# Seven of 22 gated pairs by a seven-product scheme

## The chip, the cores and the metric

One Trainium2 chip, one of its cores. The time is device microseconds of one launch: 893.27 us as the median of three runs (892.84 to 893.52). PE is TensorE, which does the matmuls; DVE is VectorE, ACT ScalarE, POOL GpSimd, SP the engine whose queue issues most transfers. Each engine takes its instructions in a written order and waits on semaphores for the others.

## What is computed

A decoder block over 16 meta tokens and 512 tokens of 1024 channels: a norm, one input projection, two mixers (a gated linear recurrence and a state-space mixer), one output projection, then the gated part that the change touches, and a last norm.

```python
def conv_glu_ffn(h, w_up, conv_w, conv_b, w_down):
    u = causal_dwconv(h @ w_up, conv_w, conv_b)      # 3 taps over tokens, per channel
    gate, val = jnp.split(u, 2, axis=-1)             # 2 x 2816 channels
    return (jax.nn.silu(gate) * val) @ w_down
...
h = h + conv_glu_ffn(rmsnorm(h, norm2_w[l]), ffn_w_up[l], ffn_conv_w[l],
                     ffn_conv_b[l], ffn_w_down[l])
y = rmsnorm(h, final_norm_w)
return y[:, N_META:, :]
```

All data are float32.

## The kernel before

Channels lie on the 128 partitions, tokens along the free axis. Every product is taken in three matmuls: weights and tokens are each split into a rounded high half (`hi`, float32r, written by ACT) and the rest (`lo`, written by DVE), and wh x xh + wh x xl + wl x xh is summed in PSUM (`product`, line 181).

The up-projection has 44 output tiles of 128 channels: tile j is a gate, tile 22 + j its value, a pair. For each tile, 8 blocks of 128 input channels, 3 matmuls each, in two halves of the tokens (258 and 256 of 514: two meta tokens are kept for the taps). `conv3` (line 790) multiplies the product by the tokens' norm factor `rstd2` (`fr`, DVE), and does the three taps: one on ACT with the bias, two on DVE (`fc`). The loop at line 806 adds `silu` on ACT, the gate's product on DVE, and at once the split of the result (`ac_hi` on ACT, `ac_lo` on DVE), from which the down-projection (`down`, line 818) reads: 8 output tiles, 22 blocks, 3 matmuls of 512 tokens each, the last tile in two halves.

Weights come in 512 KB pieces through SP's queue into three buffers (`raw`), are split into three buffers each of `whi` and `wlo`, and `weights` (line 176) keeps this two pieces ahead. A buffer is taken again when its last reader is through. PSUM has two pairs of banks (`pj`) for products of 514 tokens, and four single banks (`px`).

What sets the order: the program is written once, and a scheduler with priorities lays out a fixed order for each engine. Weight preparation runs under `first()`; `evac()` ranks above it; `tc.issue_after` puts an instruction behind another on its engine.

Of the kernel before, what the change touches and what calls it, by code (L numbers as in the profile page):

```python
# [54 lines left out]
def tile_block(ctx: ExitStack, tc: tile.TileContext, xT, w_in, w_dt, w_out, w_up, w_down,  # L55
               par, consts, consti, out, dbg=None):
    nc = tc.nc
    V, A, G, PE = nc.vector, nc.scalar, nc.gpsimd, nc.tensor
# [93 lines left out]

    def raw_tiles(key):
        name = "_".join(map(str, key))
        return (wp.tile([P, KD * P], F32, tag="raw", name=f"raw_{name}", bufs=3),
                wp.tile([P, KD * P], F32R, tag="whi", name=f"whi_{name}"),
                wp.tile([P, KD * P], F32R, tag="wlo", name=f"wlo_{name}"))
# [780 lines left out]
```

## Time and profile before

| | |
|---|---|
| median of three runs | 893.27 us (892.84 to 893.52) |
| the profiled execution | 892.85 us, span 890.7 us |
| PE, DVE, ACT busy | 98%, 62%, 47% of the span |
| mean granted TensorE clock | 0.997 |
| up-projection: first matmul, last product read out from | 505.4 us, 757.4 us |

Busy time of PE is no measure of its speed, since matmuls overlap: what counts is the distance between starts. The column "idle before" of a group is the engine's idle time before those instructions, with what ended it.

### The profile page before, as it was taken

The numbers are of one execution on the slowest core, as the hardware profiler recorded it, in microseconds if no ns is written. First come the engines' busy times: TensorE is split into PE (matmuls) and PEld (weight loads), VectorE is DVE, ScalarE is ACT, GpSimd is POOL, SyncE is SP. The second block draws the span as 40 slices with busy tenths as digits, with TensorE's granted clock in tenths as the row PEclk, the third lists the DMA queues.
The fourth block names the chain that finished last, engine by engine and source line by source line (L and its number), as shares of the span: only waits on it lengthen the run. The fifth ranks groups of instructions, "written<-read, shape, count | busy, mean of one in ns | idle before, by whom it ended". The sixth has DMA issues, their size and how long they took to land.

```text
span 890.7 us, 16334 instructions
## 1 busy us (share of the span) xinstructions
PE 871.0 (98%) x6936; PEld 831.4 (93%) x6936; DVE 553.9 (62%) x869; ACT 414.6 (47%) x625; POOL 23.8 (3%) x46
## 2 busy tenths in 40 slices
PE   7999999999999999999999999999999999999995
PEld 6998899999999999999999999999999999888885
DVE  6985968698776767454333367766666777433233
ACT  8629855866445444353222264444444444323221
POOL 1000000010000000000000000000000000000001
PEclk9999999999999999999999999999999999999998
DMA  7324332212211222244233333222232333233312
GB/s 245 91 96 163 125 97 71 72 48 70 71 58 67 95 72 72 84 153 145 95 96 95 95 93 96 84 88 93 95 96 95 96 95 90 83 88 107 89 43 94
DMA packets 29081, 84.65 MB, mean 95 GB/s; under 512 B 3128, under 2 KB 6712, under 8 KB 29008
## 3 DMA queue, kind: packets, MB, share of 16 engines
q1 hardware_dynamic: 26480, 80.02, 28.8%
q10 hardware_dynamic: 2528, 3.60, 1.3%
q8 instruction: 54, 0.88, 0.4%
q14 instruction: 19, 0.16, 0.1%
HBM read 81.45 MB, written 2.15 MB: 94 GB/s over the span
## 4 chain that ended last, share of the span: by engine, by line
PE 84%; ACT 4%; DVE 3%; DMA 1%; issue 1%; SPq 0%; DVEq 0%; ACTq 0%
PE pup L190 28%; PE pj L190 24%; PE pout L190 10%; PE pdn L823 5%; PE pdn L825 5%; PE pdn L824 5%; ACT L L467 1%; PE psu L441 1%; PE po L704 1%; PE po L703 1%; PE pa L686 1%; PE pS L674 1%; DMA ab<-acum_d 1%; DMA rs_d<-rh 1%; PE psx L429 1%
## 5 line engine op out<-in xcount | busy, mean ns | idle before, releaser
L190 PE MATMUL pj<-u_hi,whi_in 128*128 128x272 f32 (+1 forms) x752 | 156.1, 287 | 2.1 <-ACT z L512 1.4
L190 PE MATMUL pj<-u_hi,wlo_in 128*128 128x272 f32 (+1 forms) x752 | 156.6, 287 | 0.0
L190 PE MATMUL pj<-u_lo,whi_in 128*128 128x272 f32 (+1 forms) x752 | 155.9, 286 | 0.0
L190 PE MATMUL pup<-u2h,wlo_up 128*128 128x258 f32 x704 | 141.6, 282 | 0.0
L190 PE MATMUL pup<-u2h,whi_up 128*128 128x258 f32 x704 | 140.7, 282 | 0.0
L190 PE MATMUL pup<-u2l,whi_up 128*128 128x258 f32 x704 | 140.6, 281 | 0.0
L190 PEld LDWEIGHTS pj<-u_hi,whi_in 128*128 128x128 f32 x752 | 115.7, 188 | 5.2 <-issue 2.5
L190 PEld LDWEIGHTS pj<-u_lo,whi_in 128*128 128x128 f32 x752 | 116.0, 188 | 2.0 <-issue 1.5
L190 PEld LDWEIGHTS pj<-u_hi,wlo_in 128*128 128x128 f32 x752 | 116.5, 189 | 1.3 <-issue 1.2
L190 PEld LDWEIGHTS pup<-u2h,wlo_up 128*128 128x128 f32 x704 | 108.0, 188 | 0.1
L190 PEld LDWEIGHTS pup<-u2l,whi_up 128*128 128x128 f32 x704 | 108.0, 189 | 0.0
L190 PEld LDWEIGHTS pup<-u2h,whi_up 128*128 128x128 f32 x704 | 107.6, 188 | 0.0
L161 DVE TENSOR_TENSOR wlo_in<-raw_in,whi_in 128x1024 fp32r<-128x1024 f32 (+1 forms) x58 | 64.3, 1109 | 54.3 <-ACT whi_in L160 53.8
L160 ACT ACTIVATE whi_in<-raw_in 128x1024 fp32r<-128x1024 f32 (+1 forms) x58 | 56.0, 965 | 54.4 <-PE pj L190 41.0
L823 PE MATMUL pdn<-ac_hi,whi_dn 128*128 128x512 f32 (+1 forms) x198 | 73.1, 369 | 0.0
L824 PE MATMUL pdn<-ac_lo,whi_dn 128*128 128x512 f32 (+1 forms) x198 | 73.0, 368 | 0.0
L825 PE MATMUL pdn<-ac_hi,wlo_dn 128*128 128x512 f32 (+1 forms) x198 | 72.8, 368 | 0.0
L160 ACT ACTIVATE whi_up<-raw_up 128x1024 fp32r<-128x1024 f32 x44 | 46.7, 1061 | 48.9 <-PE pup L190 32.3
L801 DVE SCALAR_TENSOR_TENSOR fc<-fr,pt,fc 128x512 f32<-128x512 f32 x88 | 66.0, 749 | 2.5 <-ACT fc L799 0.9
L161 DVE TENSOR_TENSOR wlo_up<-raw_up,whi_up 128x1024 fp32r<-128x1024 f32 x44 | 53.9, 1226 | 14.8 <-ACT whi_up L160 14.8
L161 DVE TENSOR_TENSOR wlo_dn<-raw_dn,whi_dn 128x1024 fp32r<-128x1024 f32 (+1 forms) x24 | 27.3, 1137 | 57.4 <-ACT whi_dn L160 57.4
L797 DVE TENSOR_TENSOR fr<-pup,rstd 128x514 f32<-128x514 f32 x44 | 30.5, 693 | 47.5 <-PE pup L190 43.5
...
## 6 DMA issues: line engine op xcount, KB each, us to landing
raw_in<-in_w_in_dram SPq DMA_DIRECT2D x50, 512.0 KB, 3.5
raw_up<-in_w_up_dram SPq DMA_DIRECT2D x44, 512.0 KB, 3.6
raw_out<-in_w_out_dram SPq DMA_DIRECT2D x16, 512.0 KB, 3.7
raw_dn<-in_w_down_dram SPq DMA_DIRECT2D x16, 512.0 KB, 3.5
...
```

The source lines that it names most:

```text
L160: A.activation(hi[:, d], raw[:, d], AF.Copy)
L161: eng.tensor_tensor(lo[:, d], raw[:, d], hi[:, d].bitcast(F32), ALU.subtract)
L190: PE.matmul(ps[:, O + a0:O + a1], w, x[:, a0:a1], start=s, stop=e)
L429: PE.transpose(psx[0:n, t * P:(t + 1) * P], xs[t][:, a0:a1], ident)
L441: PE.matmul(psu[:], btk[0:n, b * P:(b + 1) * P], xdc[b][0:n, :], start=True, stop=True)
L467: A.activation(L[:, a0:a1], ab[:, a0:a1], AF.Relu, bias=acm[:, b, h:h + 1], scale=-1.0)
L674: PE.matmul(pS[:, b * P:(b + 1) * P], kt[:, (b - 1) * P:b * P], vt[:, (b - 1) * P:b * P], start=True, stop=True)
L797: V.tensor_tensor(r[:, T0:], ps[:, O + T0:O + NT], rstd2[:, T0:], ALU.mult)
L801: V.scalar_tensor_tensor(c[:], r[:, META - s:NT - s], col(C_FW + (2 - s) * 44 + j), c[:], ALU.mult, ALU.add)
L823: PE.matmul(ps, wh, xh, start=k0 + k == 0, stop=False)
L824: PE.matmul(ps, wh, xl, start=False, stop=False)
L825: PE.matmul(ps, wl, xh, start=False, stop=k0 + k == KF - 1)
```

## The change

Pairs 0 to 7 stay as they are ("U"). Behind them seven pairs ("W": 8, 10, 12, 13, 15, 17, 18) are computed by a Strassen-like scheme, and seven ("N") plainly on tokens that are already normed. For a W pair the 8 input blocks are halved into 4 + 4 and the tokens into two stretches of 258 that overlap by two; 7 products of 4 blocks take the place of 8. Its weights need sums of quarters (`s1`, `s2`, `rv += rg`, `rg += s2`) before they are split: seven half-width pieces `w0`, `w2`, `w1`, `s4` where a plain pair has four. The tokens need sums `t1` to `t4` for each of 4 pairs of blocks, all split (`normed_tokens`, 8 steps, each behind one gate of pairs 0 to 7). The products land in single banks (`p1`, `p2`, `p6`) and in two bank pairs (`p75`, `p43`), and DVE adds them into the gate `sg` and the negated value `sv`. N pairs read their taps from PSUM, without `fr`. The gated results `ac` keep a buffer of their own; all 22 splits are queued behind the gate of pair 19 on DVE.

```diff
+KINDS = "UUUUUUUUWNWNWWNWNWWNNN"
+HT = 258
...
-        chunks += [(("up", j), w_up[j], KD), (("up", KF + j), w_up[KF + j], KD)]
+        if KINDS[j] == "W":
+            chunks += [(("w0", j), w_up[j], KD), (("w2", j), w_up[KF + j], KD), (("w1", j), None, KD)]
+        else:
+            chunks += [(("up", j), w_up[j], KD), (("up", KF + j), w_up[KF + j], KD)]
...
+    def scheme_weights(key, src):
+        kind, j = key
+        if kind == "w0":
+            sums[j] = [raw_tile(key)]
+            nc.sync.dma_start(sums[j][0][:], src)
+            hi, lo = split_tiles(key)
+            split_weights(sums[j][0], hi, lo, slice(0, 2 * HK), V)
+            return hi, lo
+        if kind == "w2":
+            rg, rv = sums[j][0], raw_tile(key)
+            nc.sync.dma_start(rv[:], src)
+            s1, s2 = slot(f"s1_{j}", 512, tag="ab"), slot(f"s2_{j}", 512, tag="ab")
+            V.tensor_tensor(s1[:], rv[:, 0:HK], rv[:, HK:], ALU.add)
+            V.tensor_tensor(s2[:], s1[:], rg[:, 0:HK], ALU.add)
+            sums[j] += [rv, s2]
+            hi, lo = split_tiles(key)
+            split_half(s1[:], hi[:, 0:HK], lo[:, 0:HK])
+            split_half(s2[:], hi[:, HK:], lo[:, HK:])
+            return hi, lo
+        rg, rv, s2 = sums.pop(j)
+        V.tensor_tensor(rv[:, 0:HK], rv[:, 0:HK], rg[:, 0:HK], ALU.add)
+        V.tensor_tensor(rg[:, HK:], rg[:, HK:], s2[:], ALU.add)
+        hi, lo = split_tiles(key)
+        split_weights(rv, hi, lo, slice(0, 2 * HK), V)
+        h4, l4 = slot(f"s4h_{j}", 512, F32R, tag="ab"), slot(f"s4l_{j}", 512, F32R, tag="ab")
+        split_half(rg[:, HK:], h4[:], l4[:])
+        return hi, lo, h4, l4
...
+    def normed_tokens(i):
+        k = i // 2
+        if i % 2 == 0:
+            fs[k] = []
+            for kk in (k, k + KD // 2):
+                t = slot(f"n{kk}", tag="z")
+                V.scalar_tensor_tensor(t[:, T0:], hs[kk][:, T0:], col(C_N2 + kk), rstd2[:, T0:], ALU.mult, ALU.mult)
+                tag = "b0" if kk % 4 < 2 else "b1"
+                hi, lo = slot(f"n{kk}_hi", dtype=F32R, tag=tag), slot(f"n{kk}_lo", dtype=F32R, tag=tag)
+                split_half(t[:, T0:], hi[:, T0:], lo[:, T0:])
+                nh[kk], nl[kk] = hi, lo
+                fs[k] += [t[:, c] for c in tails]
+            return
+        b11, b12, b21, b22 = fs[k]
+        t13, t24 = slot(f"t13_{k}", tag="ab"), slot(f"t24_{k}", tag="ab")
+        t1, t3, t2, t4 = t13[:, 0:HT], t13[:, HT:2 * HT], t24[:, 0:HT], t24[:, HT:2 * HT]
+        V.tensor_tensor(t1, b11, b12, ALU.subtract)
+        V.scalar_tensor_tensor(t2, b22, -1.0, t1, ALU.mult, ALU.subtract)
+        V.tensor_tensor(t3, b22, b12, ALU.subtract)
+        V.scalar_tensor_tensor(t4, t2, -1.0, b21, ALU.mult, ALU.subtract)
+        ts.append([])
+        for n, t in enumerate((t1, t2, t3, t4)):
+            d = slot(f"t{n + 1}_{k}", 2 * HT, F32R)
+            split_half(t, d[:, 0:HT], d[:, HT:])
+            ts[-1].append((d[:, 0:HT], d[:, HT:]))
...
+    def taps(c, r, j, w, b):
+        n = c.shape[-1]
+        def at(s):
+            return r[..., 2 - s:2 - s + n] if len(r.shape) == 2 else r[:, :, 2 - s:2 - s + n]
+        A.activation(c, at(0), AF.Identity, bias=b, scale=w[2])
+        for s in (1, 2):
+            V.scalar_tensor_tensor(c, at(s), w[2 - s], c, ALU.mult, ALU.add)
...
-        r = slot(f"fr{j}", tag="pr")
-        V.tensor_tensor(r[:, T0:], ps[:, O + T0:O + NT], rstd2[:, T0:], ALU.mult)
+        r = ps[:, O + T0:O + NT]
         c = slot(f"fc{j}", 512, tag="pr")
-        A.activation(c[:], r[:, META:], AF.Identity, bias=col(C_FB + j), scale=col(C_FW + 88 + j))
-        for s in (1, 2):
-            V.scalar_tensor_tensor(c[:], r[:, META - s:NT - s], col(C_FW + (2 - s) * 44 + j), c[:],
-                                   ALU.mult, ALU.add)
+        with evac():
+            if kind == "U":
+                t = slot(f"fr{j}", tag="pr")
+                V.tensor_tensor(t[:, T0:], r, rstd2[:, T0:], ALU.mult)
+                r = t[:, T0:]
+            taps(c[:], r, j, taps_of(j), col(C_FB + j))
...
+    def scheme(j):
+        p1, p2, p6 = (bank(f"p{n}_{j}")[:, 0:HT] for n in (1, 2, 6))
+        p75, p43 = banks2(f"p75_{j}"), banks2(f"p43_{j}")
...
+        def mul(ps, hi, lo, xs):
+            for k, (xh, xl) in enumerate(xs):
+                wh, wl = hi[:, k * P:(k + 1) * P], lo[:, k * P:(k + 1) * P]
+                PE.matmul(ps, wh, xh, start=k == 0, stop=False)
+                PE.matmul(ps, wh, xl, start=False, stop=False)
+                PE.matmul(ps, wl, xh, start=False, stop=k == H - 1)
...
+        hi, lo = weights("w0", j)
+        mul(p1, hi[:, 0:HK], lo[:, 0:HK], b11)
+        mul(p2, hi[:, HK:], lo[:, HK:], b21)
+        hi, lo = weights("w2", j)
+        mul(p6, hi[:, HK:], lo[:, HK:], t2)
+        mul(p75[:, 512:512 + HT], hi[:, 0:HK], lo[:, 0:HK], t1)
+        hi, lo, h4, l4 = weights("w1", j)
+        mul(p75[:, 0:HT], hi[:, 0:HK], lo[:, 0:HK], t3)
+        mul(p43[:, 512:512 + HT], h4, l4, b22)
+        mul(p43[:, 0:HT], hi[:, HK:], lo[:, HK:], t4)
+        with evac():
+            A.activation(sg[:, A_], p1, AF.Copy)
+            V.tensor_tensor(sv[:, A_], sg[:, A_], p6, ALU.add)
+            V.tensor_tensor(sg[:, A_], sg[:, A_], p2, ALU.add)
+            V.tensor_tensor(by_halves(su), sv[:, A_].unsqueeze(1).broadcast_to([P, 2, HT]), two(p75), ALU.add)
+            V.tensor_tensor(sv[:, B_], su[:, A_], p75[:, 512:512 + HT], ALU.add)
+            V.tensor_tensor(sv[:, A_], su[:, A_], p43[:, 0:HT], ALU.add)
+            V.tensor_tensor(sg[:, B_], su[:, B_], p43[:, 512:512 + HT], ALU.add)
+        for c, r, i in ((cs[0], sg, j), (cs[1], sv, KF + j)):
+            w = taps_of(j) if r is sg else [ntap[:, n * KF + j:n * KF + j + 1] for n in range(3)]
+            taps(by_halves(c), by_halves(r), i, w, col(C_FB + i))
...
+    acs = []
+    for j in range(KF):
+        if KINDS[j] == "W":
+            c, c2 = scheme(j)
+            silu = A.activation(c[:], c[:], AF.Silu)
+        else:
+            c = conv3(j, KINDS[j])
+            silu = A.activation(c[:], c[:], AF.Silu)
+            c2 = conv3(KF + j, KINDS[j])
+        ac = slot(f"ac{j}", 512, tag="fqv" if j < 6 else "bc" if j < 8 else "u")
+        gate = V.tensor_tensor(ac[:], c2[:], c[:], ALU.mult)
+        acs.append(ac)
+        if j < KD:
+            with tc.issue_after(gate.ins):
+                normed_tokens(j)
+        if j == KF - 3:
+            late = gate
     ah, al = [], []
-    for j in range(KF):
-        c = conv3(j)
-        silu = A.activation(c[:], c[:], AF.Silu)
-        c2 = conv3(KF + j)
-        V.tensor_tensor(c2[:], c2[:], c[:], ALU.mult)
-        tag = ["b0"] * 4 + ["b1"] * 4 + ["m"] * 8 + ["ab"] * 2 + ["fqv"] * 2 + ["bc"] * 2
+    tag = ["z"] * 2 + ["bc", "fqv"] + ["ab"] * 2 + ["m"] * 8 + ["b0"] * 4 + ["b1"] * 4
+    for j, ac in enumerate(acs):
         hi, lo = slot(f"ac{j}_hi", 512, F32R, tag=tag[j]), slot(f"ac{j}_lo", 512, F32R, tag=tag[j])
-        A.activation(hi[:], c2[:], AF.Copy)
-        V.tensor_tensor(lo[:], c2[:], hi[:].bitcast(F32), ALU.subtract)
+        with tc.issue_after(late.ins):
+            split_half(ac[:], hi[:], lo[:])
```

DVE at the start of pair 9, before: what stands between the product `pup8` and pair 9 (`fr` reads a product, `wlo_up` is a weight's low half, `fc` the taps).

```order
L797 TENSOR_TENSOR fr8_6943<-pup8_6894,rstd2_5856 128x514
L161 TENSOR_TENSOR wlo_up_31_6952<-raw_up_31_6950,whi_up_31_6951 128x1024
L801 SCALAR_TENSOR_TENSOR fc8_6945<-fr8_6943,pt_75,fc8_6945 128x512 x2
L797 TENSOR_TENSOR fr30_7005<-pup30_6956,rstd2_5856 128x514
L161 TENSOR_TENSOR wlo_up_10_7018<-raw_up_10_7016,whi_up_10_7017 128x1024
L801 SCALAR_TENSOR_TENSOR fc30_7007<-fr30_7005,pt_75,fc30_7007 128x512 x2
L810 TENSOR_TENSOR fc30_7007<-fc30_7007,fc8_6945 128x512
L814 TENSOR_TENSOR ac8_lo_7013<-fc30_7007,ac8_hi_7012 128x512
```

DVE from the last of pair 8's weights to the release of its first bank pair, with the change (`s4l`: low half of the seventh weight piece; `t2` to `t4`: low halves of token sums; `s1`, `s2`, `raw_w2`: sums of pair 10's weights; `sv`, `sg`, `su`: read-out of pair 8).

```order
L180 TENSOR_TENSOR s4l_8_7011<-raw_w0_8_6845,s4h_8_7010 128x512
L180 TENSOR_TENSOR t2_3_6985<-t24_3_6977,t2_3_6985 128x258
L180 TENSOR_TENSOR t3_3_6988<-t13_3_6976,t3_3_6988 128x258
L180 TENSOR_TENSOR t4_3_6991<-t24_3_6977,t4_3_6991 128x258
L196 TENSOR_TENSOR s1_10_7188<-raw_w2_10_7186 128x512
L197 TENSOR_TENSOR s2_10_7189<-s1_10_7188,raw_w0_10_7126 128x512
L204 TENSOR_TENSOR raw_w2_10_7186<-raw_w2_10_7186,raw_w0_10_7126 128x512
L954 TENSOR_TENSOR sv8_7000<-sg8_6999,p6_8_6996 128x258
L955 TENSOR_TENSOR sg8_6999<-sg8_6999,p2_8_6995 128x258
L956 TENSOR_TENSOR su8_7001<-sv8_7000,p75_8_6997 128x516
L173 TENSOR_TENSOR wlo_up_31_7070<-raw_up_31_7068,whi_up_31_7069 128x1024
L957 TENSOR_TENSOR sv8_7000<-su8_7001,p75_8_6997 128x258
```

The read-out of a product was the next thing behind its end; now three adds on the weights of pair 10 and a weight's low half stand inside pair 8's read-out.

DVE around the second last pair, before: each product's read-out, two taps and the pair's one split.

```order
L797 TENSOR_TENSOR fr20_8479<-pup20_8430,rstd2_5856 128x514
L161 TENSOR_TENSOR wlo_up_43_8488<-raw_up_43_8486,whi_up_43_8487 128x1024
L801 SCALAR_TENSOR_TENSOR fc20_8481<-fr20_8479,pt_75,fc20_8481 128x512 x2
L797 TENSOR_TENSOR fr42_8541<-pup42_8492,rstd2_5856 128x514
L161 TENSOR_TENSOR wlo_dn_0_0_8554<-raw_dn_0_0_8552,whi_dn_0_0_8553 128x1024
L801 SCALAR_TENSOR_TENSOR fc42_8543<-fr42_8541,pt_75,fc42_8543 128x512 x2
L810 TENSOR_TENSOR fc42_8543<-fc42_8543,fc20_8481 128x512
L814 TENSOR_TENSOR ac20_lo_8549<-fc42_8543,ac20_hi_8548 128x512
L797 TENSOR_TENSOR fr21_8607<-pup21_8558,rstd2_5856 128x514
```

DVE behind the gate of pair 19 with the change, from the fifth split on (`fc20` is the product of pair 20, read from PSUM).

```order
L180 TENSOR_TENSOR ac1_lo_8806<-ac1_6128,ac1_hi_8805 128x512
L180 TENSOR_TENSOR ac5_lo_8822<-ac5_6688,ac5_hi_8821 128x512
L180 TENSOR_TENSOR ac7_lo_8830<-ac7_6974,ac7_hi_8829 128x512
L173 TENSOR_TENSOR wlo_up_43_8621<-raw_up_43_8619,whi_up_43_8620 128x1024
L180 TENSOR_TENSOR ac3_lo_8814<-ac3_6408,ac3_hi_8813 128x512
L890 SCALAR_TENSOR_TENSOR fc20_8614<-pup20_8565,pt_75,fc20_8614 128x512
L180 TENSOR_TENSOR ac8_lo_8834<-ac8_7124,ac8_hi_8833 128x512
L180 TENSOR_TENSOR ac9_lo_8838<-ac9_7251,ac9_hi_8837 128x512
L180 TENSOR_TENSOR ac10_lo_8842<-ac10_7383,ac10_hi_8841 128x512
L180 TENSOR_TENSOR ac11_lo_8846<-ac11_7510,ac11_hi_8845 128x512
L180 TENSOR_TENSOR ac12_lo_8850<-ac12_7648,ac12_hi_8849 128x512
L890 SCALAR_TENSOR_TENSOR fc20_8614<-pup20_8565,pt_75,fc20_8614 128x512
```

Five splits have moved between the two taps that read the same product, and eight more splits and a weight's low half stand ahead of the first.

SP's queue of weight transfers at pairs 8 to 10, before.

```order
L169 DMA raw_up_8_6760<-in_w_up_dram 128x1024
L169 DMA raw_up_30_6822<-in_w_up_dram 128x1024
L169 DMA raw_up_9_6888<-in_w_up_dram 128x1024
L169 DMA raw_up_31_6950<-in_w_up_dram 128x1024
L169 DMA raw_up_10_7016<-in_w_up_dram 128x1024
```

The same place with the change.

```order
L188 DMA raw_w0_8_6845<-in_w_up_dram 128x1024
L194 DMA raw_w2_8_6907<-in_w_up_dram 128x1024
L223 DMA raw_up_9_7038<-in_w_up_dram 128x1024
L223 DMA raw_up_31_7068<-in_w_up_dram 128x1024
L188 DMA raw_w0_10_7126<-in_w_up_dram 128x1024
L194 DMA raw_w2_10_7186<-in_w_up_dram 128x1024
```

The pieces and their sizes are the same; pair 8's two raw pieces now stay in their buffers until the sums are split.

## Rows read from the trace of the kernel before

**Rows 1.** The page: busy share of each engine; shares of the chain that ended last.

```profile
PE 871.0 (98%) x6936; PEld 831.4 (93%) x6936; DVE 553.9 (62%) x869; ACT 414.6 (47%) x625; POOL 23.8 (3%) x46
...
PE pup L190 28%; PE pj L190 24%; PE pout L190 10%; PE pdn L823 5%; PE pdn L825 5%; PE pdn L824 5%; ACT L L467 1%; PE psu L441 1%; PE po L704 1%; PE po L703 1%; PE pa L686 1%; PE pS L674 1%; DMA ab<-acum_d 1%; DMA rs_d<-rh 1%; PE psx L429 1%
```

**Rows 2.** Waits of PE: who waited, for whom, total us, times, longest.

```profile
PE pj L190 <- ACT z L512: 1.4, 1, 1.4
```

**Rows 3.** Windows, 560 to 580: length, PE, PEld, DVE, ACT, POOL, clock, DMA, GB/s.

```profile
560.00:580.00 20.00, 20.00 (x171) 20.00 (x170) 13.50 (x18) 8.07 (x10) 0.00 (x0) 1.00 0.35 106
```

**Rows 4.** Timeline of DVE, 569 to 581: start, us, operation, idle before.

```profile
569.12 0.69 DVE L797 TENSOR_TENSOR fr<-pup,rstd 128x514 f32<-128x514 f32 x1
569.98 1.22 DVE L161 TENSOR_TENSOR wlo_up<-raw_up,whi_up 128x1024 fp32r<-128x1024 f32 x1 [0.16 <-ACT whi_up L160]
571.12 1.53 DVE L801 SCALAR_TENSOR_TENSOR fc<-fr,pt,fc 128x512 f32<-128x512 f32 x2
...
574.83 0.69 DVE L797 TENSOR_TENSOR fr<-pup,rstd 128x514 f32<-128x514 f32 x1 [2.18 <-PE pup L190]
...
579.78 0.69 DVE L814 TENSOR_TENSOR ac_lo<-fc,ac_hi 128x512 fp32r<-128x512 f32 x1 [0.70 <-ACT ac_hi L813]
580.54 0.69 DVE L797 TENSOR_TENSOR fr<-pup,rstd 128x514 f32<-128x514 f32 x1
```

**Rows 5.** The page's groups: matmuls of the up-projection.

```profile
L190 PE MATMUL pup<-u2h,wlo_up 128*128 128x258 f32 x704 | 141.6, 282 | 0.0
```

**Rows 6.** Timeline of PE in the last down product.

```profile
865.79 0.28 PE L823 MATMUL pdn<-ac_hi,whi_dn 128*128 128x256 f32 x1
...
870.36 0.28 PE L823 MATMUL pdn<-ac_hi,whi_dn 128*128 128x256 f32 x1
```

**Rows 7.** Groups by line and shape: count, busy us, mean ns.

```profile
L801 DVE SCALAR_TENSOR_TENSOR fc<-fr,pt,fc 128x512 f32<-128x512 f32 x88 | 66.0, 749 | 2.5 <-ACT fc L799 0.9
...
L161 DVE TENSOR_TENSOR wlo_up<-raw_up,whi_up 128x1024 fp32r<-128x1024 f32 x44 | 53.9, 1226 | 14.8 <-ACT whi_up L160 14.8
...
L160 ACT ACTIVATE whi_up<-raw_up 128x1024 fp32r<-128x1024 f32 x44 | 46.7, 1061 | 48.9 <-PE pup L190 32.3
...
L799 ACT ACTIVATE fc<-fr,pt 128x512 f32<-128x512 f32 x44 | 35.9, 816 | 1.5 <-DVE fr L797 1.4
...
L653 DVE TENSOR_TENSOR kBC<-k,sd 128x256 f32<-128x256 f32 x8 | 3.4, 420 | 0.0
...
L865 DVE SCALAR_TENSOR_TENSOR ot<-xr,pt,rs 128x256 f32<-128x256 f32 x2 | 0.9, 472 | 0.0
```

**Rows 8.** Timeline of DVE, two instructions in a full queue.

```profile
523.89 0.69 DVE L810 TENSOR_TENSOR fc<-fc,fc 128x512 f32<-128x512 f32 x1
524.50 0.69 DVE L797 TENSOR_TENSOR fr<-pup,rstd 128x514 f32<-128x514 f32 x1
```

**Rows 9.** The page: weight transfers, us from issue to landing.

```profile
raw_up<-in_w_up_dram SPq DMA_DIRECT2D x44, 512.0 KB, 3.6
```

**Rows 10.** Timeline of PE at its first matmuls.

```profile
6.12 0.81 PE L190 MATMUL pj_b<-v_hi,whi_in 128*128 128x272 f32 x2 [6.12 <-ACT v_hi L216]
6.72 0.65 PE L190 MATMUL pj_c<-v_hi,whi_in 128*128 128x272 f32 x2
7.16 0.64 PE L190 MATMUL pj_b<-v_lo,whi_in 128*128 128x272 f32 x2
...
11.08 0.40 PE L190 MATMUL pj_c<-v_hi,wlo_in 128*128 128x272 f32 x2
11.32 0.40 PE L190 MATMUL pj_b<-v_hi,whi_in 128*128 128x272 f32 x2
```

**Rows 11.** PE's last matmuls, and windows behind them.

```profile
881.93 0.70 PE L857 MATMUL psn<-fsq,cf 128*128 128x256 f32 x2 [0.96 <-ACT fsq L853]
...
884.00:885.00 1.00, 0.00 (x0) 0.00 (x0) 1.00 (x3) 0.00 (x0) 1.00 (x2) 0.91 0.00 0
885.00:886.00 1.00, 0.00 (x0) 0.00 (x0) 1.00 (x2) 0.00 (x0) 0.50 (x1) 0.50 0.43 147
```

More of the change, by code (lines that the diff above doesn't have):

```diff
@@ L151, in tile_block, with raw_tile, split_tiles @@
     wnext = [0]
+    def raw_tile(key):
+        return wp.tile([P, KD * P], F32, tag="raw", name="raw_" + "_".join(map(str, key)), bufs=3)
+    def split_tiles(key):
+        name = "_".join(map(str, key))
+        return (wp.tile([P, KD * P], F32R, tag="whi", name=f"whi_{name}"),
+                wp.tile([P, KD * P], F32R, tag="wlo", name=f"wlo_{name}"))
     def raw_tiles(key):
[L154 to L157, printed above, removed]
+        return (raw_tile(key),) + split_tiles(key)
     def split_weights(raw, hi, lo, d, eng):
@@ L161, in split_weights, with split_half @@
         eng.tensor_tensor(lo[:, d], raw[:, d], hi[:, d].bitcast(F32), ALU.subtract)
+    HK = KD * P // 2
+    sums = {}
+    def split_half(x, hi, lo):
+        A.activation(hi, x, AF.Copy)
+        V.tensor_tensor(lo, x, hi.bitcast(F32), ALU.subtract)
+    def scheme_weights(key, src):
[25 more added lines that the diff above has]
+        return hi, lo, h4, l4
     def ahead(n):
@@ L165, in ahead @@
             key, src, kc = chunks[wnext[0]]
+            if key[0] in ("w0", "w1", "w2"):
+                with first():
+                    wdone[key] = scheme_weights(key, src)
+                wnext[0] += 1
+                continue
             with first():
@@ L787, in second_norm @@
         log_exp(rstd2, parts, T0, 1.0 / DM)
-    def conv3(j):
+    ntap = cp.tile([P, 3 * KF], F32, name="ntap")
+    for i in range(3):
+        V.tensor_scalar(ntap[:, i * KF:(i + 1) * KF], pt[:, C_FW + i * 2 * KF + KF:C_FW + (i + 1) * 2 * KF],
+                        -1.0, None, ALU.mult)
+    tails = (slice(T0, T0 + HT), slice(NT - HT, NT))
+    nh, nl, ts = [None] * KD, [None] * KD, []
+    fs = {}
+    def normed_tokens(i):
[23 more added lines that the diff above has]
+            ts[-1].append((d[:, 0:HT], d[:, HT:]))
@@ L791, in conv3, with taps_of @@
+    def taps(c, r, j, w, b):
[5 more added lines that the diff above has]
+            V.scalar_tensor_tensor(c, at(s), w[2 - s], c, ALU.mult, ALU.add)
+    def taps_of(j):
+        return [col(C_FW + i * 2 * KF + j) for i in range(3)]
+    def conv3(j, kind):
         w = weights("up", j)
         ps = banks2(f"pup{j}")
-        product([(ps, w)], u2h, u2l, T0, KD)
+        if kind == "U":
+            product([(ps, w)], u2h, u2l, T0, KD)
+        else:
+            product([(ps, w)], nh, nl, T0, KD)
@@ L803, in conv3 @@
-        return c
-    ah, al = [], []
-    for j in range(KF):
-        c = conv3(j)
-        silu = A.activation(c[:], c[:], AF.Silu)
-        c2 = conv3(KF + j)
-        V.tensor_tensor(c2[:], c2[:], c[:], ALU.mult)
-        tag = ["b0"] * 4 + ["b1"] * 4 + ["m"] * 8 + ["ab"] * 2 + ["fqv"] * 2 + ["bc"] * 2
+        with evac():
+            if kind == "U":
+                t = slot(f"fr{j}", tag="pr")
+                V.tensor_tensor(t[:, T0:], r, rstd2[:, T0:], ALU.mult)
+                r = t[:, T0:]
+            taps(c[:], r, j, taps_of(j), col(C_FB + j))
@@ new lines, in conv3, with two, by_halves @@
+        return c
+    def scheme(j):
+        p1, p2, p6 = (bank(f"p{n}_{j}")[:, 0:HT] for n in (1, 2, 6))
+        p75, p43 = banks2(f"p75_{j}"), banks2(f"p43_{j}")
+        H = KD // 2
+        b11 = [(nh[k][:, tails[0]], nl[k][:, tails[0]]) for k in range(H)]
+        b21 = [(nh[k][:, tails[0]], nl[k][:, tails[0]]) for k in range(H, KD)]
+        b22 = [(nh[k][:, tails[1]], nl[k][:, tails[1]]) for k in range(H, KD)]
+        t1, t2, t3, t4 = ([t[n] for t in ts] for n in range(4))
+        def mul(ps, hi, lo, xs):
[4 more added lines that the diff above has]
+                PE.matmul(ps, wl, xh, start=False, stop=k == H - 1)
+        sg, sv, su = (slot(f"s{n}{j}", 2 * HT, tag=t) for n, t in (("g", "L"), ("v", "L"), ("u", "pr")))
+        cs = [slot(f"fc{i}", 512, tag="pr") for i in (j, KF + j)]
+        A_, B_ = slice(0, HT), slice(HT, 2 * HT)
+        def two(ps):
+            return ps[:].rearrange("p (a t) -> p a t", a=2)[:, :, 0:HT]
+        def by_halves(t):
+            return t[:].rearrange("p (a t) -> p a t", a=2)
+        hi, lo = weights("w0", j)
[19 more added lines that the diff above has]
+            taps(by_halves(c), by_halves(r), i, w, col(C_FB + i))
+        return cs
@@ new lines, in tile_block @@
+    acs = []
[3 more added lines that the diff above has]
+            silu = A.activation(c[:], c[:], AF.Silu)
+        else:
+            c = conv3(j, KINDS[j])
[9 more added lines that the diff above has]
+            late = gate
```

## The prediction

> **What bounds the kernel now.** I read the page's busy shares and chain first: TensorE (PE) is busy 98% of the span and the chain that ended last is matmuls for most of its length, 28% of it those of the up-projection [rows 1]. Then who waits: PE's waits after its first matmul are few, the longest 1.4 us [rows 2]. So time is PE's instruction stream, and another engine counts only where it holds PE up. A stretch in the middle of the up-projection shows the room beside it: PE 20.0 of 20 us, VectorE (DVE) 13.5, ScalarE (ACT) 8.1 [rows 3]. DVE's own order of time repeats with every pair of a gate and a value product: `fr` begins at 569.12 and again at 580.54, so a pair takes PE 11.42 us and one product 5.71; between them DVE waits about 2.2 us for PE and 0.7 us for ACT [rows 4]. A bank pair of `pj` that is not read out within 5.71 us of its product's end stops PE, and so does a weight split that is late.
>
> **What PE saves.** The up-projection has 3 x 704 matmuls [rows 5], 96 in a pair. A scheme pair has 7 products x 4 blocks x 3 = 84, each of 258 columns. With the weights changing in the same pattern (wh, wh, wl) the last down product runs 39 matmuls of 256 columns in 870.36 - 865.79 = 4.57 us [rows 6], 0.117 each, 0.118 for 258: 84 x 0.118 = 9.92 us, 1.50 less than 11.42. By the pair's own pitch (11.42 / 96 = 0.119) it is 1.39. Seven pairs: 9.7 to 10.5; I take **-10.1 us**.
>
> **What DVE gains in work.** Durations [rows 4, 7]: add or split 1.23 us for 1024 elements, 0.69 for 512, 0.42 for 256 (taken for 258), a tap 0.75 (0.47 for 256); ACT 1.06 for 1024 and 0.82 for a tap with bias. In a full queue the next instruction starts 0.61 us after one of 0.69 [rows 8] and 1.14 after one of 1.23 [rows 4], so each hides about 0.08.
> Plain pairs 0 to 7: 8.2 us of DVE before; minus the moved split 0.69, plus the normed tokens (2 x 0.75 + 2 x 0.69) in even pairs, the sums (6 x 0.42 + 2 x 0.47) in odd ones: 10.4 and 11.0 of 11.42. Costed at nothing: the waits of [rows 4] hide it. If that cover goes, PE stops only once the lag passes 5.71 us. The three negated taps and ACT's share (its 8.1 of 20 us leave more than half free) cost nothing either.
> A scheme pair: 4 weight adds (2.8), five low halves (2 x 1.23 + 3 x 0.69 = 4.5), one read-out of 516 and five of 258 (2.8), 4 taps (3.0), gate (0.7): 13.8 us for 9.9 of PE. A later plain pair has 2 x 1.23 + 4 x 0.75 + 0.69 = 6.2 for 11.42. W and N together fit (20.0 of 21.3), so on the mean DVE is not the bound; the hand-offs are.
>
> **Hand-off 1, pair 8.** Let Z be the end of pair 7's first product; PE begins pair 8 at Z + 5.7. From `fr7` at Z + 0.1 DVE has 22 instructions to the end of `s4l_8`: 4 x 0.69 (`fr`, gate) + 2 x 0.75 (`n3`, `n7`) + 5 x 0.69 (splits) + 4 x 0.75 (taps) + 2 x 1.23 (`wlo_w1_8`, `wlo_up_9`) + 3 x 0.42 + 2 x 0.47 (sums) = 15.4, less 21 x 0.08, plus about 0.6 of waits for ACT: `s4l_8` ends at Z + 14.4 (13.8 to 15.4). The last tokens' first sum is ready 2.1 us before that, its high half on ACT at Z + 12.9. PE wants it 42 matmuls into the pair, at Z + 10.6. It waits 2.3 us, then 0.5 for `s4h_8`, and ends the pair at Z + 18.4 instead of Z + 15.6: **+2.8**.
> Then the order puts `s1_10`, which reads the raw weights `w2` of pair 10, ahead of pair 8's read-out. Three raw buffers exist; `up_31` and `w0_10`, read only further down, hold two, so `raw_w2_10` gets the third when `s4l_8` has read `raw_w0_8`. A transfer lands 3.6 us after its issue [rows 9]. DVE stands still from Z + 15.5 to Z + 18.1, and behind the waiting `s1_10` stand two more adds (2.0 with it), `sv`, `sg`, `su` (1.5), `wlo_up_31` (1.15) and the second `sv` (0.45), which frees the bank pair for `pup9`: Z + 23.2 against PE's Z + 18.4, **+4.8**. With the ends of `s4l_8` the two together cost 7.0 to 8.6; I take **+7.6**. PE does four matmuls of pair 10 in that pause.
>
> **Hand-off 2, the next scheme's `s1` ahead of a read-out.** The same stands before the read-outs of pairs 10, 13 and 15. There the transfer waits for a plain weight's low half, 3.6 us before the landing; followed the same way, the second `sv` ends 0.1, 0.9 and 0.1 us after PE is through; in pairs 12, 17 and 18 no transfer stands before it. **+1.1**, 0 to 2.5.
>
> **Hand-off 3, the splits at the end.** They may begin behind pair 19's gate, which ends 4.6 us after that pair's last product. Up to the second tap of `fc20` DVE has 13 splits (0.61 each, 7.9), `wlo_up_43` (1.14) and 2 taps (1.4): 10.5 us, so 15.1 after that product. Pair 21's first product wants this bank pair 2 x 5.71 = 11.4 after it: **+3.7** (3.0 to 4.8, by 0.55 to 0.69 for a split). Behind that the down stage starts with all it needs: the last split is due only at its 63rd matmul.
>
> **The clock.** At the start, after 6.1 us without work, PE's pairs of matmuls stand 0.44 us apart (its 1.2 GHz pace) from 6.72, and 0.24 apart from 11.08 on (2.4 GHz): 22 matmuls at the slow pace lose about 2.2 us [rows 10]. At the end PE's last matmul is over at 882.63; the granted clock reads 0.91 for 884 to 885 and 0.50 behind it [rows 11], so it falls at about 884.8, 2.2 us later. The pauses at pair 9 (4.8 us with four matmuls in it) and at pair 21 (3.7 us) are longer than that, the one in pair 8 about as long. I take one fall: **+2.2** (0 to 4.4).
> The Trainium skill (TensorE: Matmul & The Clock Gate, section "HAM oscillation — how this bites in real kernels") says that an engine which waits between bursts of matmuls goes back to its lower clock each time it does so for long. No run here shows it in mid-kernel. By that rule both long pauses fall and the sum would be 2.2 us higher; by a reading in which only an engine out of work falls, 2.2 us lower.
>
> **Sum.** -10.1 + 7.6 + 1.1 + 3.7 + 2.2 = +4.5 on the profiled execution's 892.85 us (span 890.7) gives 897.35. That execution lies 0.42 under the median, 893.27, so the forecast is **897.8 us**.
>
> **Rivals.**
> A, the clock holds. The stalls are as summed, PE comes back at full pace: 892.85 + 2.3 + 0.4 = 895.6 (893.5 to 896.5). For it: no fall in mid-kernel before, where no wait is over 1.4 us. Against it: the fall after 2.2 us at the end.
> B, faster. The fixed part of DVE's instructions hides wholly. 0.42 for 256 and 1.23 for 1024 leave 0.15 that no element explains; I let 0.08 hide. At 0.16, `s4l_8` ends 1.9 us sooner and the read-out 0.6 sooner after it: pair 8 costs 5.0, the tail 2.4, hand-off 2 about 0.5, the pauses are near 2.2 us or in two pieces and the clock holds: -10.1 + 7.9 = -2.2, 891.1. It decides where a split of 512 in a full queue is followed after 0.53 us and not 0.61. [Rows 8] and [rows 4] speak against it.
> C, DVE bounds the whole scheme part. Lags add up over W W (27.6 us of DVE for 19.8 of PE) instead of being worked off, each scheme pair loses 1 to 2 us, and the clock falls twice: 901 to 905. For it: 13.8 against 9.9 in each pair. Against it: 6.2 against 11.42 in the pair behind.
>
> **How the numbers follow.** The forecast's case (895.5 to 900.5) gets 0.42, A 0.22, B 0.17, C 0.14; 0.05 lies on something not read. Apart 0.2% (1.8 us) a change can be told from none: under 891.5 is B, 0.17; 891.5 to 895.1 is the lower part of A, the upper edge of B and half of what was not read, 0.16; above it 0.67. The range that holds eight in ten reaches into B and C: 889.0 to 903.0; the bounds of the terms alone give 892.8 (-10.5 + 7.0 + 0 + 3.0, no fall) to 903.9 (-9.7 + 8.6 + 2.5 + 4.8 + 4.4).
>
> **What would show it.** PE has 84 matmuls less, and those of `p75` and `p43` are about 0.118 apart. In PE's waits: `p75` on ACT's high half of the last sum or on `s4h`, 2 to 3 us once; `pup` on DVE's `sv`, 4 to 5 us at pair 9; `pup` on DVE's tap `fc`, 3 to 4.5 us at pair 21. In DVE's: `s1` on the DMA of `raw_w2`, about 2.6 us at pair 10's weights. A slice with a granted clock under 1 behind one of these pauses. It is wrong if PE's waits in the up-projection sum to under 8 us, if the clock reads 1.00 and pitches stay 0.118 throughout, or if waits stand in every scheme pair.

## The result: 896.06 us, 0.41% slower

The changed kernel takes 896.06 us (median of 9 runs, 894.14 to 899.23); the kernel before takes 892.84 beside it. The ratio is 1.0041, with a 95% interval of 1.0031 to 1.0052. The forecast was 897.8, in a range of 889.0 to 903.0. The profiled execution took 898.56 us, span 896.8, so it is one of the longer ones: the four of the nine above 898 us have a mean granted clock (the share of full speed that TensorE was granted, over the span) of 0.989 to 0.991, the five others one of 0.993 to 0.995.

The page of the changed kernel, its busy shares and the engines' shares of its chain, which answer to [rows 1]:

```profile
PE 869.4 (97%) x6852; PEld 828.8 (92%) x6852; DVE 595.0 (66%) x983; ACT 432.2 (48%) x677; POOL 23.8 (3%) x46
...
PE 81%; DVE 5%; ACT 4%; DMA 2%; issue 1%; SPq 0%; DVEq 0%; ACTq 0%
```

The same shares of the chain before:

```profile
PE 84%; ACT 4%; DVE 3%; DMA 1%; issue 1%; SPq 0%; DVEq 0%; ACTq 0%
```

PE has 84 matmuls less, as was counted, and a share of 97% where it had 98%: the span grew although the work shrank. DVE has 41 us more, and in the chain it stands with 5% where it had 3%. So time is in waits. PE's waits within the up-projection, where the kernel before has none:

```profile
PE p L927 <- ACT t L179: 2.0, 1, 2.0
PE pup L244 <- DVE sv L957: 2.0, 2, 1.2
PE pup L244 <- DVE fc L890: 1.7, 1, 1.7
PE p L927 <- ACT whi_w L172: 1.1, 1, 1.1
PE pdn L996 <- ACT whi_dn L172: 1.0, 1, 1.0
```

Three of these are the pauses that the prediction named: on ACT's half of a token sum (`t`), on `sv`, on `fc`. The two others lie within the same pauses: `whi_w` is the weight of the four matmuls of pair 10 that PE does there, `whi_dn` that of two down matmuls. Where they stand shows in PE's order of time (start, duration, operation, idle before):

```profile
602.43 0.28 PE L929 MATMUL p<-t,wlo_w 128*128 128x258 f32 x1
604.70 0.39 PE L927 MATMUL p<-t,whi_w 128*128 128x258 f32 x1 [1.99 <-ACT t L179]
605.22 0.39 PE L927 MATMUL p<-n_hi,s4h 128*128 128x258 f32 x1
...
611.66 0.28 PE L929 MATMUL p<-t,wlo_w 128*128 128x258 f32 x1
613.02 0.38 PE L927 MATMUL p<-n_hi,whi_w 128*128 128x258 f32 x1 [1.08 <-ACT whi_w L172]
...
613.48 0.28 PE L928 MATMUL p<-n_lo,whi_w 128*128 128x258 f32 x1
614.95 0.47 PE L244 MATMUL pup<-n_hi,whi_up 128*128 128x258 f32 x2 [1.18 <-DVE sv L957]
...
669.08 0.28 PE L929 MATMUL p<-t,wlo_w 128*128 128x258 f32 x1
670.14 0.47 PE L244 MATMUL pup<-n_hi,whi_up 128*128 128x258 f32 x2 [0.78 <-DVE sv L957]
...
746.07 0.40 PE L244 MATMUL pup<-n_hi,wlo_up 128*128 128x258 f32 x2
747.43 0.50 PE L996 MATMUL pdn<-ac_hi,whi_dn 128*128 128x512 f32 x1 [0.96 <-ACT whi_dn L172]
747.77 0.39 PE L997 MATMUL pdn<-ac_lo,whi_dn 128*128 128x512 f32 x1
749.83 0.77 PE L244 MATMUL pup<-n_hi,whi_up 128*128 128x258 f32 x2 [1.67 <-DVE fc L890]
750.40 0.63 PE L244 MATMUL pup<-n_lo,whi_up 128*128 128x258 f32 x2
750.82 0.63 PE L244 MATMUL pup<-n_hi,wlo_up 128*128 128x258 f32 x2
```

A matmul of this size starts 0.12 us after the one before. From 602.43 to 604.70 PE has lost 2.15 us to the last token sum, and 0.40 more to `s4h`. From 611.66 to 613.02 it loses 1.24, from 613.48 to 614.95 1.35, with four matmuls of pair 10 in between; at 669.08 0.94, behind pair 13. At pair 21 it stands still from 746.07 to 749.83 but for two down matmuls: 3.5 us, 3.1 net of these. DVE at the same places:

```profile
591.99 0.69 DVE L909 TENSOR_TENSOR fr<-pup,rstd 128x514 f32<-128x514 f32 x1 [1.24 <-PE pup L244]
...
605.46 0.69 DVE L180 TENSOR_TENSOR s4l<-raw_w,s4h 128x512 fp32r<-128x512 f32 x1
...
609.92 0.69 DVE L196 TENSOR_TENSOR s<-raw_w 128x512 f32<-128x512 f32 x1 [2.76 <-DMA raw_w<-in_w_up_dram]
...
612.65 0.69 DVE L956 TENSOR_TENSOR su<-sv,p 128x516 f32<-128x516 f32 x1
613.25 1.22 DVE L173 TENSOR_TENSOR wlo_up<-raw_up,whi_up 128x1024 fp32r<-128x1024 f32 x1
614.39 0.42 DVE L957 TENSOR_TENSOR sv<-su,p 128x258 f32<-128x258 f32 x1
...
745.27 0.75 DVE L890 SCALAR_TENSOR_TENSOR fc<-pup,pt,fc 128x512 f32<-128x512 f32 x1
745.93 3.09 DVE L180 TENSOR_TENSOR ac_lo<-ac,ac_hi 128x512 fp32r<-128x512 f32 x5
748.94 0.74 DVE L890 SCALAR_TENSOR_TENSOR fc<-pup,pt,fc 128x512 f32<-128x512 f32 x1
```

`s1` waits 2.76 us for its transfer, with the read-out behind it, and the `sv` of 614.39 ends where PE's `pup` starts. At the end, the second tap of `fc20` at 748.94 stands behind five splits, just as the order had them; it ends at 749.68, and PE starts at 749.83.

And the clock (columns as in [rows 3]; the column before the last two is the granted clock):

```profile
606.00:608.00 2.00, 2.00 (x11) 2.00 (x10) 1.16 (x4) 0.09 (x1) 0.00 (x0) 0.50 0.51 98
...
616.00:618.00 2.00, 2.00 (x12) 2.00 (x11) 2.00 (x4) 1.13 (x3) 0.00 (x0) 0.50 0.58 221
...
748.00:750.00 2.00, 0.33 (x2) 0.20 (x2) 2.00 (x4) 0.84 (x3) 0.00 (x0) 0.76 0.00 0
750.00:752.00 2.00, 2.00 (x10) 2.00 (x11) 2.00 (x4) 0.35 (x1) 0.00 (x0) 0.50 0.28 25
...
754.00:756.00 2.00, 2.00 (x12) 2.00 (x11) 0.00 (x0) 0.00 (x0) 0.00 (x0) 0.53 0.03 8
```

Three times the clock is at 0.50, that is 1.2 instead of 2.4 GHz, each time at a pause, and for unlike lengths: about 3.4 us from 605.7, 3.4 us from 615.9 and 6.8 us from 749.1. The first two begin 1 us after PE has gone on, the third 0.8 us before. In these stretches pairs of matmuls start 0.42 to 0.43 us apart (750.40 and 750.82 above) and not 0.24. PE loses 1.4 us in the first stretch, 1.4 in the second and 2.8 in the third: 5.6 us in this execution. The pause of 0.94 us behind pair 13 has no fall behind it.

What PE saves shows in pair 15, which has no wait in it: from its first matmul to that of pair 16

```profile
681.62 0.28 PE L927 MATMUL p<-n_hi,whi_w 128*128 128x258 f32 x1
...
691.77 0.48 PE L244 MATMUL pup<-n_hi,whi_up 128*128 128x258 f32 x2
```

are 10.15 us, where a plain pair takes 11.42 to 11.50: 1.3 us a pair, 9.1 for seven (pairs 17 and 18 take 20.20 together, by which it is 9.5). The profiled execution adds up to within half a microsecond: -9.1 + 2.55 (tokens, `s4h`) + 2.59 (pair 9) + 0.94 (behind pair 13) + 3.1 (pair 21) + 5.6 (clock) = +5.7, and it took 898.56 - 892.85 = 5.71 us more (its span 6.1 more). Without the clock the same sum is +0.1: the waits take back the whole saving, and what the kernel loses is the clock's.

### The profile page after: what moved, and what is told of

Read it like the earlier page. It is cut to its first block, busy times and chain, and to the rows that moved or that the text cites. A ratio compares the mean times of both kernels' runs of the same rounds, so it can differ in the third digit from the quotient of the medians.

```text
span 896.8 us, 16326 instructions
## 1 busy us (share of the span) xinstructions
PE 869.4 (97%) x6852; PEld 828.8 (92%) x6852; DVE 595.0 (66%) x983; ACT 432.2 (48%) x677; POOL 23.8 (3%) x46
## 3 DMA queue, kind: packets, MB, share of 16 engines
HBM read 81.45 MB, written 2.15 MB: 93 GB/s over the span
## 4 chain that ended last, share of the span: by engine, by line
PE 81%; DVE 5%; ACT 4%; DMA 2%; issue 1%; SPq 0%; DVEq 0%; ACTq 0%
PE pj L244 24%; PE pup L244 19%; PE pout L244 10%; PE pdn L998 5%; PE pdn L997 5%; PE pdn L996 5%; PE p L928 2%; PE p L927 2%; PE p L929 2%; ACT L L521 1%; DMA raw_w<-in_w_up_dram 1%; PE psu L495 1%; DVE ac_lo L180 1%; PE po L758 1%; PE po L757 1%
## 5 line engine op out<-in xcount | busy, mean ns | idle before, releaser
L172 ACT ACTIVATE whi_dn<-raw_dn 128x1024 fp32r<-128x1024 f32 (+1 forms) x24 | 23.7, 988 | 82.3 <-PE pdn L997 67.6
L172 ACT ACTIVATE whi_up<-raw_up 128x1024 fp32r<-128x1024 f32 x30 | 31.8, 1061 | 59.2 <-PE pup L244 25.3
L244 PE MATMUL pup<-u2h,wlo_up 128*128 128x258 f32 (+1 forms) x256 | 51.7, 283 | 0.0
L244 PE MATMUL pup<-u2l,whi_up 128*128 128x258 f32 (+1 forms) x256 | 51.2, 281 | 0.0
L244 PE MATMUL pup<-u2h,whi_up 128*128 128x258 f32 (+1 forms) x256 | 51.1, 282 | 0.0
L244 PE MATMUL pup<-n_hi,whi_up 128*128 128x258 f32 x224 | 47.0, 293 | 3.6 <-DVE sv L957 2.0
L244 PE MATMUL pup<-n_lo,whi_up 128*128 128x258 f32 x224 | 46.6, 291 | 0.0
L173 DVE TENSOR_TENSOR wlo_up<-raw_up,whi_up 128x1024 fp32r<-128x1024 f32 x30 | 36.7, 1223 | 14.7 <-ACT whi_up L172 14.7
L244 PE MATMUL pup<-n_hi,wlo_up 128*128 128x258 f32 x224 | 46.4, 290 | 0.0
L996 PEld LDWEIGHTS pdn<-ac_hi,whi_dn 128*128 128x128 f32 x198 | 37.2, 188 | 7.8 <-ACT whi_dn L172 1.2
```

What stands on the lines that cost most here:

```text
L996: PE.matmul(ps, wh, xh, start=k0 + k == 0, stop=False)
```

## The experiments

Each one is timed in five rounds against the kernel before, on one chip per group (before: 893.20 for experiments 1 to 4, 892.93 for 5 to 8); there are 11 runs each of experiments 1, 2, 3 and 5, five of 4, 6 and 7, and four of 8. The theory: the change saves PE 9 to 10 us, and gives it back in the hand-offs at pairs 8, 9 and 21 and in the falls of the clock behind them. The rival: DVE has too much work in all of the scheme part, and a wait taken away at one place comes back at the next.

**1. Splits behind the gate of pair 20.**

```diff
-        if j == KF - 3:
+        if j == KF - 2:
             late = gate
```

> The 22 splits are queued behind the gate of pair 20 instead of pair 19; nothing else. Theory (the splits stand ahead of fc20's second tap and hold the bank pair of pair 21, and the pause lets TensorE's clock fall): the wait of pup on DVE fc (1.7 us by the profile, 3.1 us of PE's time net of the two down matmuls done in it) and the slow stretch behind it (14 pairs of matmuls at 0.43 instead of 0.24 us, 2.7 us) go; up to 5.8 us less than the changed kernel's profiled 898.56, less than that against its median of 896.06, as its clock need not fall in every run: 890.5 us (889 to 892). Rival (the splits are DVE work that only moves, and the down stage waits for them instead): 894 to 896.5, with waits of pdn on ac_hi or ac_lo.

893.33 us (890.66 to 895.05), ratio to before 1.0000 (0.9991 to 1.0010): 2.7 us less than the changed kernel, where 5.6 were expected. The waits on `fc` and `whi_dn` are gone, and between 740 and 885 us no slice has a clock under 1.00. The profiled execution gained 5.2 us (893.35 against 898.56), near what the theory counted there; the medians gained half of that. So the wait is as described, and the expected median was wrong. The mean clocks of the runs say where: the profiled executions have 0.990 and 0.993, but the median over the runs is 0.993 for both kernels. So the median gained about the wait (3.1 us) and nothing of the clock; why the other runs' clock did not gain is not shown. The down stage did not wait for the splits.

**2. Pairs 8 and 9 changed about.**

```diff
-KINDS = "UUUUUUUUWNWNWWNWNWWNNN"
+KINDS = "UUUUUUUUNWWNWWNWNWWNNN"
```

> Pair 8 is plain on normed tokens, pair 9 by the scheme; seven scheme pairs as before, so tokens' sums of the last step have a pair more until they are read. Theory (pair 8 loses 2.5 us to the last token sums and s4h, and 1.4 us to the clock that falls behind it): both go; 892 us (890.5 to 894). The wait of s1 for the transfer stays somewhere at the next scheme pair, smaller, as two scheme pairs now follow each other and the second starts in single banks. Rival (DVE has more work than PE in every scheme pair, and the lag only shows one pair later): 895 to 898, with a like wait at pair 9 or 10.

891.26 us (889.26 to 893.55), ratio 0.9979 (0.9969 to 0.9989). The token wait is gone and nothing came back in its place but two short waits for a weight's high half. In its up-projection the one slow stretch is the one behind pair 21, of 3.4 us, where the pause is the same 3.5 us:

```profile
744.00:746.00 2.00, 0.35 (x3) 0.38 (x4) 2.00 (x4) 0.85 (x2) 0.00 (x0) 1.00 0.00 0
746.00:748.00 2.00, 2.00 (x15) 2.00 (x14) 2.00 (x4) 0.17 (x1) 0.00 (x0) 0.65 0.29 45
748.00:750.00 2.00, 2.00 (x11) 2.00 (x11) 1.25 (x2) 0.00 (x0) 0.00 (x0) 0.50 0.60 225
750.00:752.00 2.00, 2.00 (x19) 2.00 (x19) 0.00 (x0) 0.00 (x0) 0.00 (x0) 1.00 0.00 0
```

This execution, the longest of its eleven, has another one earlier, in a stage that the change leaves alone: 3.4 us from 302.9, behind a single wait of 1.36 us (`mt` is a small operand of one of the mixers). So "only slow stretch", which is said of it ahead of experiment 6, is true of the up-projection alone.

```profile
301.84 0.38 PE L754 MATMUL pm<-mt 128*128 128x2 f32 x2 [1.36 <-DVE mt L745]
...
304.00:306.00 2.00, 2.00 (x11) 2.00 (x11) 1.94 (x4) 0.00 (x0) 0.00 (x0) 0.50 0.23 86
```

**3. The next scheme's `s1` behind the read-out.** `readout` is the last add of a scheme pair's read-out.

```diff
+            with ExitStack() as st:
+                if readout:
+                    st.enter_context(tc.issue_after(readout[-1].ins))
-            V.tensor_tensor(s1[:], rv[:, 0:HK], rv[:, HK:], ALU.add)
+                V.tensor_tensor(s1[:], rv[:, 0:HK], rv[:, HK:], ALU.add)
```

> The first sum of a scheme pair's weights (s1, and with it what reads it) is queued on DVE behind the last add of the read-out of the scheme pair before; nothing else. Theory (s1_10 waits 2.8 us for its transfer with the read-out of pair 8 behind it): the wait of pup on sv after pair 8 (1.35 us of PE's time) and the second slow stretch (1.45 us) go, and the 0.8 us at pair 14; PE's wait of 1.2 us for the high half of pair 10's first weight stays, as four matmuls of pair 10 still stand ahead of pup9: 893 us (891.5 to 895). The token wait of 2 us and the first slow stretch are still there. Rival (the read-out would be late without the transfer too, as DVE is behind): 895 to 897, PE waiting for sv as before.

894.63 us (892.71 to 895.98), ratio 1.0015 (1.0006 to 1.0024). DVE now waits for PE at pair 8's read-out, and not for the transfer:

```profile
609.74 0.42 DVE L958 TENSOR_TENSOR sv<-sg,p 128x258 f32<-128x258 f32 x1 [3.47 <-PE p L933]
...
612.28 0.41 DVE L961 TENSOR_TENSOR sv<-su,p 128x258 f32<-128x258 f32 x1
...
613.28 0.68 DVE L200 TENSOR_TENSOR s<-raw_w 128x512 f32<-128x512 f32 x1
```

PE's wait for `sv` there and the second slow stretch are gone. The gain is only 1.4 us in the median: the new order also put four matmuls of pair 15 ahead of `pup14`, and PE waits 1.4 us for their weight, where it waited 0.8 us before, and 0.4 us for `sv` behind pair 18. By the starts of its matmuls PE's waits are only 0.3 us shorter in all than the changed kernel's (8.9 against 9.2 us); the rest is the clock's, whose mean is 0.995 in the median of the runs where it was 0.993.

**4. All three.**

> All three edits together. Theory: what is left is PE's saving of 10.1 us and about 1 us of small waits, and no slow stretch: 884 us (882.5 to 887), granted clock 0.997 as in the kernel before. Rival (waits are set by DVE's load and the clock falls at another place): 889 to 893, clock 0.994 or lower.

885.84 us (885.56 to 887.07), ratio 0.9921 (0.9909 to 0.9934): faster than both kernels. In the up-projection two waits are left, and the mean clock is 0.998:

```profile
PE p L931 <- ACT whi_w L172: 1.1, 1, 1.1
PE pup L248 <- DVE sv L961: 0.4, 1, 0.4
```

Against the changed kernel's 896.06 the single edits gained 2.7, 4.8 and 1.4 us, 9.0 together; all three gained 10.2. The rival falls: DVE has the same instructions as in the changed kernel, and no wait took the place of those removed.

**5. The same without a scheme pair.**

```diff
-KINDS = "UUUUUUUUNWWNWWNWNWWNNN"
+KINDS = "UUUUUUUU" + "N" * 14
```

> Experiment 4 with all 14 pairs behind the eighth plain, on normed tokens: no scheme pair, 84 matmuls more; the tokens' sums, which nothing reads then, are still computed. Theory (the scheme saves PE 1.4 us a pair and nothing else of the change touches the time once no wait is left): 885.84 + 9.8 - 1.5 (the small waits of experiment 4, which stand at scheme pairs) = 894 us (892.5 to 895). Rival (normed tokens, taps from PSUM and late splits save something by themselves, or the scheme's saving is smaller): 888 to 891.

893.37 us (892.41 to 894.40), ratio 1.0003 (0.9994 to 1.0012), with no wait of PE in the up-projection. Taps from PSUM, normed tokens, their sums and the late splits are worth nothing where PE is the bound and no wait stands. The scheme is worth 7.5 us in experiment 4 (timed on the other chip), 9.4 with the 1.8 us that PE still stands still there (1.24 at 628, 0.60 at 715).

**6. Fillers in the pause at pair 21.** Experiment 2, with 24 matmuls that nothing reads between pairs 20 and 21.

```diff
+            fp = bank("fill")
+            with tc.issue_after(lastmm[0].ins):
+                for i in range(24):
+                    fm = PE.matmul(fp[:, 0:HT], nh[i % KD][:, T0:T0 + P], nh[i % KD][:, T0:T0 + HT], ...)
+            with tc.issue_after(fm.ins):
+                product([(ps, w)], nh, nl, T0, KD)
```

> Experiment 2 (whose only slow stretch stands behind the pause at pair 21, 746.4 to 750 in its profile) with 24 matmuls of 258 columns, whose result nothing reads, queued on PE between the products of pairs 20 and 21, where it stands still for about 3.4 us but for two down matmuls; 24 x 0.12 = 2.9 us, so they end before DVE releases the bank pair. Theory (the pause itself is DVE's and stays, the clock falls because PE stands still): no slow stretch at pair 21, 1.7 us less than 891.26: 889.6 us (889 to 890.5), and less spread between runs. Rival (the clock falls for another reason, or not often): 891 to 894, as the fillers cost 0 to 2.9 us.

889.41 us (888.86 to 889.59), ratio 0.9959 (0.9947 to 0.9972): 1.85 us less than experiment 2, with 24 matmuls more. The pause is filled, the product of pair 21 starts when DVE lets it, and it starts at full pace; the clock stays at 1.00:

```profile
738.91 3.03 PE L907 MATMUL fill<-n_hi 128*128 128x258 f32 x24
741.78 0.39 PE L1006 MATMUL pdn<-ac_hi,whi_dn 128*128 128x512 f32 x1
...
742.43 0.47 PE L246 MATMUL pup<-n_hi,whi_up 128*128 128x258 f32 x2
```

and the windows of that stretch:

```profile
742.00:744.00 2.00, 1.98 (x15) 1.60 (x14) 2.00 (x4) 0.63 (x1) 0.00 (x0) 1.00 0.03 8
744.00:746.00 2.00, 2.00 (x19) 2.00 (x18) 1.90 (x4) 0.00 (x0) 0.00 (x0) 1.00 0.76 215
```

So the loss behind the pause is the clock's and not a part of the wait, and it is PE's standing still that lets it fall. The five runs lie within 0.73 us, where the eleven of experiment 2 spread over 4.3. Not every run of experiment 2 has the fall: three have a mean clock of 0.997, as experiment 6 has at most, and take 889.56 to 889.87 us. So the fillers buy what a run without the fall has anyway.

**7. PE's order kept.** Experiment 4; `lastmm` is the last matmul of the product before, and the down products are treated alike.

```diff
-        mul(p1, hi[:, 0:HK], lo[:, 0:HK], b11)
+        with tc.issue_after(lastmm[0].ins):
+            mul(p1, hi[:, 0:HK], lo[:, 0:HK], b11)
```

> Experiment 4 with PE's order kept: a scheme pair's first product, and the down products, are queued behind the last matmul of the product before, so that no four matmuls of the next scheme pair and no down matmul stand inside a pair. Theory (PE's wait of 1.1 us for the high half of a weight in experiment 4 is due to these four matmuls, whose weight buffer is only free later): 1.1 to 1.5 us less, 884.5 us (883.8 to 885.3). Rival (the wait only moves to the next product): 885.8.

885.69 us (885.29 to 887.43), ratio 0.9923 (0.9910 to 0.9935): no gain. The rival was right, the wait only moved: PE waits 1.2 us for `sv` at 628 where it waited 1.1 us for `whi_w`.

**8. Eight scheme pairs.** Experiment 7 with one more.

```diff
-KINDS = "UUUUUUUUNWWNWWNWNWWNNN"
+KINDS = "UUUUUUUUNWWNWWNWWNWWNN"
```

> Experiment 7 with eight scheme pairs (9, 10, 12, 13, 15, 16, 18, 19), two and two with a plain one between. Theory (DVE is not the bound with one more: 8 x 13.8 + 6 x 6.2 = 147.6 us of work in 8 x 10.05 + 6 x 11.42 = 148.9 of PE, and starts that overlap by 0.08 leave more): 1.4 us less than experiment 7, 883.1 us (882.5 to 884.5). Rival (DVE is full, its lag grows from pair to pair): 885 to 890, PE waiting for sv at the later pairs and the clock falling there.

885.05 us (884.89 to 885.66), ratio 0.9913 (0.9898 to 0.9928): 0.6 us less than experiment 7, half of what PE saves in a pair, half a microsecond above what the theory allowed and at the lower edge of the rival's range; the lowest median of all, though its ratio's interval overlaps those of experiments 4 and 7. PE waits for `sv` three times, 1.9 us together, and in the stretches of two scheme pairs DVE is busy for 94 to 97% of the time:

```profile
609.00:630.50 21.50, 20.32 (x170) 20.12 (x169) 20.81 (x34) 12.34 (x17) 0.00 (x0) 1.00 0.39 124
...
642.00:662.20 20.20, 20.20 (x170) 20.20 (x169) 19.38 (x30) 10.40 (x14) 0.00 (x0) 1.00 0.37 112
673.60:694.30 20.70, 20.41 (x170) 20.22 (x169) 19.39 (x31) 10.89 (x16) 0.00 (x0) 1.00 0.36 122
705.80:726.60 20.80, 20.37 (x170) 20.17 (x169) 19.46 (x31) 12.05 (x18) 0.00 (x0) 1.00 0.34 112
```

DVE does not bound the kernel yet, but it has little left, as the rival had it.

## Why the prediction was right, step by step

**What bounds the kernel.** PE's stream and the hand-offs, as said: with the three waits out (experiment 4) it is faster than before by 7.4 us.

**PE's saving.** -10.1 was forecast, 9.1 came. The step that was off is the pace: 0.118 us for a matmul of 258 columns was taken from down matmuls of 256, but in scheme pairs they stand 0.120 to 0.121 apart (20.20 us for the 168 of pairs 17 and 18, 10.15 for the 84 of pair 15).

**Hand-off 1.** Right by mechanism and, for DVE, almost to the tenth. With the end of pair 7's first product at 591.9 (`fr` follows it at 591.99), `s4l_8` was to end at 606.3 and ended at 606.15; `s1_10` was to begin at 610.0 and began at 609.92; the `sv` that frees the bank was to end at 615.1 and ended at 614.8. The first wait took 2.55 us where 2.8 stood. The second took 2.6 where 4.8 stood, and that term was mis-sized: PE came 1.5 us later than forecast, since the clock had fallen within pair 8, where the sum had put no fall, and the four matmuls of pair 10, which the text names, were not taken off. Experiments 2 and 3 show both waits apart.

**Hand-off 2.** +1.1 was forecast, +0.94 came, behind pair 13 and nowhere else, as worked out.

**Hand-off 3.** +3.7 was forecast, +3.1 came net of the two down matmuls. Experiment 1 takes it away by moving the splits one gate down.

**The clock.** The step that was taken too low for the profiled execution: one fall of 2.2 us was forecast, and three came, worth 5.6. The Trainium skill (TensorE: Matmul & The Clock Gate, section "HAM oscillation — how this bites in real kernels") has an engine that waits between bursts go back to its lower clock each time it waits for long. The trace agrees that it falls at waits: the three falls stand at pauses of 2.15 us, of 1.24 and 1.35 us with four matmuls between, and of 3.5 us. It does not bear out "each time", nor that the length of the pause decides alone. Single pauses of 0.94 to 1.5 us in the up-projections, in experiments 3 and 4 too, have none behind them, and neither has a wait of 1.2 to 1.3 us for `mt` at 209 us in all ten traces; the wait of 1.36 us in experiment 2 has one, and three of its runs have, by their mean clock, none behind the 3.5 us at pair 21. Across runs the sum is smaller: the median lies 2.5 us below the profiled execution, at a mean clock of 0.993.

Against the profiled execution the sum was 1.2 us short: 1.0 too much saved, 3.2 too much for the waits, 3.4 too little for the clock. Against the median it was 1.7 us long. So that it came out close is partly errors that cancel. One of its own signs of being wrong nearly held: it was to be wrong if PE's waits in the up-projection sum to under 8 us, and the view of waits has 7.8; by the starts of the matmuls, as the terms were counted, they are 9.2. The waits on `sv` and `fc` stand there with 1.2 and 1.7 us, where 4 to 5 and 3 to 4.5 were named, since the matmuls of pair 10 and of the down stage divide both pauses.

Rival A falls with the slow stretches, though the median of 896.06 lies in the range that A had, 893.5 to 896.5: the time alone would not have told the two apart. Rival B named its mark, a split followed after 0.53 us: five splits in a row take 3.09 us, which is 0.60 each, so it falls. Rival C falls with experiment 4.

What stays open is why the slow stretch at the same pause is 3.4 us in the profiled execution of experiment 2 and 6.8 in that of the changed kernel, and why some runs have none.
